# Three further expert blocks computed ahead, kept in device memory until the expert sum reaches them

## The chip, the cores and the metric

The kernel runs on one core of a Trainium2 chip. The core has a matrix engine (TensorE, PE in the profile; its weight loads are PEld), a vector engine (VectorE, DVE), an activation engine (ScalarE, ACT), GpSimd (POOL) and SyncE (SP), whose queue issues nearly all transfers between the device's memory and the on-chip memory. The metric is the device time of one execution in microseconds, as the median of several runs.

## The reference, cut to what matters

One decoder layer is computed for 1024 prompt tokens and 32 sample tokens (8 sequences of 4), 1056 columns in all, at width 1024. An RWKV-7 mixer and a pooling mixer share one input projection; their outputs go through `W_out` and are added to x, which gives h. Then comes PEER, a feed-forward part with 16384 single-neuron experts: each token has 8 heads, each head picks 16 experts by product keys, and

```
act = gelu(einsum('thkd,td->thk', u_tab[expert], xn)) * gate
out = einsum('thk,thkd->td', act, v_tab[expert])
```

with `xn = rmsnorm(h)`. A gated per-layer embedding and a final norm end the layer. All in float32.

## The kernel before, in words

Features lie on the 128 partitions, tokens along the free dimension. The column order is 32 sample tokens and then 1024 prompt tokens. The columns are worked in four groups, `GROUPS = ((0, 288), (288, 544), (544, 800), (800, 1056))`.

**Two ways to the experts.** Columns 0 to 671 (`ND = 672`) are done densely: the product of all 16384 u rows with the tokens is formed, in 128 blocks of 128 experts (`EB = 128`), multiplied by a dense gate (zero for experts not chosen) that was built in memory (`g_d`) earlier, and multiplied by the v table. Columns 672 to 1055 (384 tokens, `GT`) are done by gathers: POOL fetches the chosen u and v rows and DVE multiplies and adds them (L1229, L1237, L1246).

**A float32 product from three fast ones.** Each operand is split in a high part (ACT copy to fp32r) and a rest (a subtraction), and hi·hi, hi·lo and lo·hi are added. `esplit` (L1092 to L1099) loads 512 KB of a weight block into `eraw` (3 buffers, SP), writes `ehi` (ACT, L1096) and `elo` (2 buffers each), the latter on DVE (L1098) or, where the caller passes `PTT`, on POOL (the profile shows those at line 127). `emm` (L1120) does the matmuls: 8 pieces of the contraction, three products, two halves of 336 columns, so 48 matmuls for one block.

**One u block.** `ublock(b)` does esplit, emm into a PSUM tile `pd` (2 buffers) and a Gelu on ACT (L1126) into a 672-wide tile: `OT0` to `OT7` for the first eight (`NPRE = 8`), a rotating `wt` tile (3 buffers) for the later ones. `OT0` to `OT5` are in the pool `dr`; `OT6`, `OT7`, `wt` and the gate tile `gq` are in pools that are opened only when the pool `gp` of the dense gate is closed.

**The last group is projected.** `phase_c(gi)` adds the mixers' output projection to x, giving `h` (tile `h` of the pool `work`, 128 x 8 x 288), normalises h in place, splits it (L682 and line 127) and, for the gathered tokens, transposes it on PE (L728) into `xt_d`. After that `h` is not used. Then 16 blocks of `wq` are multiplied (`mm3`, L655 to L657), the results copied to `q` (L738, tile of `work`), multiplied with the keys (L743), and the scores go to memory (L747). It has 24 steps: 8 blocks of `w_out`, 16 of `wq`. For the last group the first 18 blocks of weights come ready split from `wc_d` by SP (L644, L645, half blocks, 3 buffers `whi` and `wlo`); from block 18 (`C3E`) on they go through `esplit` with POOL.

**What stands beside it.** At step 4 the generator of the dense gate for the last dense tile, `t_stream(2)` (top-k and selection on DVE, L765 to L860; one-hots, L905 to L907; small matmuls L913; copies L914 on ACT; 2 MB stores `g_d`, L916), is written out first; then `merge` interleaves the 24 steps of `phase_c(3)` with the 8 steps of `upre`, always taking the stream with the smaller finished share (phase_c at a tie).

**What follows.** `gtop(0)` selects experts for the first 128 gathered tokens. Then the pools of `phase_c` (`ws`, `mv`, `work`) are closed and `dw` is opened in their place, with 9 buffers each of `wh` and `wl`. `dense` walks the 128 blocks: ublock if it is not there yet, then `ugate` (multiply by the gate, L1177, DVE; high part `wh`, L1179, ACT; rest `wl`, L1181, DVE). After each eight blocks `vblock` multiplies them with eight blocks of v (L1120 again), adding into OT (L1191 for the first group, L1189 later). The first v group is written out right after block 8 of u. The gather loop and the tail (the gated embedding, for dense tokens `td`, for gathered ones `tg` with the tile `GH`) follow.

The order in each engine's queue is not the program's order: a planner lists the instructions by a simulated time, with the program's order as priority, and each engine then works its list strictly in order.

Of the kernel before, what the change touches and what calls it, by code (L numbers as in the profile page):

```python
# [10 lines left out]
F32 = mybir.dt.float32  # L11
# [4 lines left out]
AF = mybir.ActivationFunctionType  # L16
# [4 lines left out]
KB = D // 128  # L21
# [21 lines left out]
ND = GB - GA  # L43
GT = T - ND
XW = T // 3
NH = ND // 2
# [17 lines left out]
def body(ctx, tc, io):  # L64
    nc = tc.nc
    mm = nc.tensor.matmul
    TT, STT, TS, ACT = (nc.vector.tensor_tensor, nc.vector.scalar_tensor_tensor, nc.vector.tensor_scalar,
                        nc.scalar.activation)

    const = ctx.enter_context(tc.tile_pool(name="const", bufs=1))  # L70
    dram = ctx.enter_context(tc.tile_pool(name="dram", bufs=1, space=bass.MemoryType.DRAM))
# [9 lines left out]
    h2_d = dram.tile([128, KB, GT], F32, name="h2_d")  # L81
    wc_d = dram.tile([KB + 16, 128, 2, KB, 128], F32, name="wc_d")
    xt_d = dram.tile([GT, D], F32, name="xt_d")
    g_d = dram.tile([EB // GQ, 128, NTC, GQ, TC], F32, name="g_d")

    def v3(ap, n):
# [358 lines left out]
    maxn = max(b - a for a, b in GROUPS)  # L445
# [478 lines left out]
    def b_stream(ca, cb, ahead=2):  # L924
        while nxt[0] < cb or any(c < cb for c, _ in active):
            c = nxt[0]
            if (c < min(cb + ahead, NCH) and len(active) < NSLOT and (not active or since[0] >= STAG)
                    and not (held[0] and c % NSLOT == 1)):
                active.append((c, bchunk(c)))
                nxt[0], since[0] = c + 1, 0  # L930
            since[0] += 1
            for a in list(active):
                try:
                    next(a[1])
                except StopIteration:
                    active.remove(a)
                yield

    def b_len(ca, cb):
        return (cb - ca) * 19  # L940
# [6 lines left out]
    def t_stream(gi):  # L947
        for t0, m in tiles_of(gi):
            if GA <= GROUPS[gi][0] + t0 < GB:
                yield from top(tk, GROUPS[gi][0] + t0, m)  # L950

    def t_len(gi):
        n = 0
        for t0, m in tiles_of(gi):
            if GA <= GROUPS[gi][0] + t0 < GB:
                n += 24 + m // GT8
        return n

    def merge(streams):
        live = [[0, n, g] for n, g in streams]  # L960
        while live:
            s = min(live, key=lambda s: s[0] / s[1])
            try:
                next(s[2])
                s[0] += 1
            except StopIteration:
                live.remove(s)
# [101 lines left out]
    work = cstack.enter_context(tc.tile_pool(name="wc", bufs=1, reuse_waits="tile"))  # L1069
# [11 lines left out]
    def xsplit():  # L1081
        return (dr.tile([128, KB, ND], F32R, name="XH"), dr.tile([128, KB, ND], F32R, name="XL"))

    NPRE = 8
    NWT = 3
    DP = ((0, NH), (NH, NH))
    U = {}

    def PD():
        return dps.tile([128, 2, 512], F32, name="pd")  # L1090

    def esplit(src, sub=TT):  # L1092
        raw = dr.tile([128, KB, 128], F32, name="eraw", bufs=3)
        nc.sync.dma_start(raw, src)
        hi = dr.tile([128, KB, 128], F32R, name="ehi", bufs=2)
        ACT(hi, raw, AF.Copy)  # L1096
        lo = dr.tile([128, KB, 128], F32R, name="elo", bufs=2)
        sub(lo, raw, hi.bitcast(F32), op=ALU.subtract)  # L1098
        return hi, lo  # L1099
# [3 lines left out]
    def otile(db):  # L1103
        if db not in OT:
            OT[db] = (dr if db < KB - 2 else late).tile([128, ND], F32, name=f"OT{db}")
        return OT[db]

    def wt_tile():
        return late.tile([128, ND], F32, name="wt", bufs=NWT)

    def halves(t):
        return t.rearrange("p (a b) -> p a b", a=2)

    def emm(ps, w, xs, parts):
        wh_, wl_ = w
        for k in range(KB):
            xh, xl = xs[k]
            for w_, x_, first, last in ((wh_, xh, k == 0, False), (wh_, xl, False, False), (wl_, xh, False, k == KB - 1)):
                for a, (s, n) in enumerate(parts):
                    mm(ps[:, a, :n], w_[:, k, :], x_[:, s:s + n], start=first, stop=last)  # L1120

    def ublock(b, sub=TT):
        ps = PD()
        emm(ps, esplit(io["uT"][b], sub), xs, DP)
        U[b] = otile(b) if b < NPRE else wt_tile()
        ACT(halves(U[b]), ps[:, :, :NH], AF.Gelu)  # L1126

    def upre():
        for b in range(NPRE):
            ublock(b, PTT)  # L1130
            yield

    CL = [0, 24, 24, 24, 24]
    for step in range(1, NG + 1):
        streams = []
        if step < NG:
            c_ = BC[step + 2:step + 4]
            streams.append((b_len(*c_), b_stream(*c_)))
        if 0 <= step - 2 < NG:
            streams.append((t_len(step - 2), t_stream(step - 2)))  # L1140
        if 0 <= step - 1 < NG:
            streams.append((CL[step], phase_c(step - 1)))
        if step == NG:
            for _ in streams[0][1]:
                pass
            gstack.close()
            late = ctx.enter_context(tc.tile_pool(name="late", bufs=1, side="right", reuse_waits="tile"))
            gqp = ctx.enter_context(tc.tile_pool(name="gqp", bufs=2, side="right", reuse_waits="tile"))
            streams = [streams[1], (NPRE, upre())]
        merge(streams)  # L1150
        if step == NG - 1:
            nc.sync.dma_start(io["wkv_p"], S[-1])
            pbx.close()
            dr = ctx.enter_context(tc.tile_pool(name="dr", bufs=1, side="right", reuse_waits="tile"))
            dps = ctx.enter_context(tc.tile_pool(name="dps", bufs=2, side="right", space=bass.MemoryType.PSUM, reuse_waits="tile"))
            XH, XL = xsplit()
            for k in range(KB):
                nc.sync.dma_start(XH[:, k, :].bitcast(F32), xh_d[:, k, :])
                nc.sync.dma_start(XL[:, k, :].bitcast(F32), xl_d[:, k, :])
            xs = [(XH[:, k, :], XL[:, k, :]) for k in range(KB)]  # L1160
# [10 lines left out]
    def ugate(b):  # L1171
        if b % GQ == 0:
            gqs[0] = gqp.tile([128, NTC, GQ, TC], F32, name="gq")
            nc.sync.dma_start(gqs[0], g_d[b // GQ])
        wt_ = U[b]
        w3 = wt_.rearrange("p (c t) -> p c t", t=TC)
        TT(w3, w3, gqs[0][:, :, b % GQ, :], op=ALU.mult)  # L1177
        wh = dw.tile([128, ND], F32R, name="wh", bufs=VG + 1)
        ACT(wh, wt_, AF.Copy)  # L1179
        wl = dw.tile([128, ND], F32R, name="wl", bufs=VG + 1)  # L1180
        TT(wl, wt_, wh.bitcast(F32), op=ALU.subtract)  # L1181
        Ws[b] = (wh, wl)

    def vblock(g, db):
        w = esplit(io["vP"][g, db])
        ps = PD()
        emm(ps, w, [Ws[b] for b in range(g * VG, (g + 1) * VG)], DP)
        if g:
            TT(halves(OT[db]), ps[:, :, :NH], halves(OT[db]), op=ALU.add)  # L1189
        else:  # L1190
            ACT(halves(OT[db]), ps[:, :, :NH], AF.Copy)  # L1191
        if g == EB // VG // 2:
            ht = wt_tile()
            nc.sync.dma_start(ht, hT_d[:, db, GA:GB])
            TT(OT[db], OT[db], ht, op=ALU.add)

    def dense(b0, b1):
        for b in range(b0, b1):
            if b < EB:
                if b not in U:  # L1200
                    ublock(b)
                ugate(b)
            if b % VG == 0 and b:
                for db in range(KB):
                    vblock(b // VG - 1, db)

    NB0 = 2 * VG + 2
    dense(0, NB0)
    for col in range(128, GT, 128):
        gtop(col)  # L1210
# [5 lines left out]
    dpt = ctx.enter_context(tc.tile_pool(name="dpt", bufs=2, space=bass.MemoryType.PSUM, reuse_waits="tile"))  # L1216

    dense(NB0, EB + 1)

    for col in range(0, GT, 128):  # L1220
# [31 lines left out]
        for half in range(2):  # L1252
            ps = dpt.tile([128, 512], F32, name="pt")
# [3 lines left out]
            o = ht[:, half * 4:half * 4 + 4, :m]  # L1257
# [184 lines left out]
def program(arrays, extra=()):  # L1442
    nc = bacc.Bacc("TRN2", target_bir_lowering=False, num_devices=1)
    io = {k: nc.dram_tensor(k, v.shape, mybir.dt.from_np(v.dtype), kind="ExternalInput").ap()
          for k, v in arrays.items()}
    for k, s in list(OUTS.items()) + list(extra):
        io[k] = nc.dram_tensor(k, s, F32, kind="ExternalOutput").ap()
    with tile.TileContext(nc, schedule_with_timeline_sim=True) as tc, ExitStack() as ctx:
        body(ctx, tc, io)
    return nc  # L1450
# [15 lines left out]
```

## Time and profile before

| | |
|---|---|
| three runs | 3265.51, 3267.89, 3258.73 us, median 3265.51 |
| the profiled execution | 3262.93 us, span 3261.2 us |
| PE | busy 3103.6 us, 95% of the span |
| DVE | busy 2584.9 us, 79% |
| POOL, ACT | busy 1391.2 us and 1109.8 us |
| granted TensorE clock, mean | 0.973 |
| transfers | 857.86 MB, mean 263 GB/s |
| the stage that is changed | about 1110 to 1325 us |
| the dense sum | about 1325 to 3146 us, then the tail |

Busy times are shares of one engine's span and overlap between engines. The profiled execution lies 2.58 us under the median of the runs. A row of a windows table gives, for a stretch of time, its length and each engine's busy time with the number of instructions, then the granted clock, the share of the DMA engines and GB/s.

### The profile page before, as it was taken

How to read it: one execution, taken by the hardware profiler on the slowest of the kernel's cores; microseconds unless marked ns; L12 is line 12 of the kernel's file. 1: busy time of each engine (PE TensorE's matmuls, PEld its weight loads, DVE VectorE, ACT ScalarE, POOL GpSimd, SP SyncE). 2: the span in 40 equal slices, each digit the busy share in tenths (PEclk: the TensorE clock that was granted, in tenths of full speed). 3: DMA queues.
4: the chain of work that ended last, by engine and by line, in shares of the span. 5: the costliest groups of instructions: out<-in, count | busy, mean ns of one | idle time of the engine just before them, and what ended most of it. 6: DMA issues, size and time to landing. Idle time of an engine off the chain costs nothing.

```text
span 3261.2 us, 66203 instructions
## 1 busy us (share of the span) xinstructions
PE 3103.6 (95%) x26807; PEld 2983.0 (91%) x26807; DVE 2584.9 (79%) x5093; ACT 1109.8 (34%) x1708; POOL 1391.2 (43%) x1069
## 2 busy tenths in 40 slices
PE   8998899989989688999999999999999999999998
PEld 7887788878878588999999999999999999999997
DVE  7776344479998995988889888888888888888955
ACT  6442323435645554322122222222212212212343
POOL 5211410020020242156666666656666666666532
PEclk9999899999999799999999999999999999999998
DMA  3326457958877868389999999999999999999823
GB/s 119 113 95 146 129 166 220 300 164 258 252 220 231 273 214 273 126 296 337 328 346 344 317 350 343 321 339 357 324 327 346 330 331 343 337 327 342 312 97 126
DMA packets 436129, 857.86 MB, mean 263 GB/s; under 512 B 109808, under 2 KB 230896, under 8 KB 431344
## 3 DMA queue, kind: packets, MB, share of 16 engines
q1 hardware_dynamic: 324560, 447.76, 42.5%
q0 software_dynamic: 111264, 405.88, 34.4%
q8 instruction: 210, 3.44, 0.4%
q14 instruction: 95, 0.78, 0.1%
HBM read 732.92 MB, written 120.60 MB: 262 GB/s over the span
## 4 chain that ended last, share of the span: by engine, by line
PE 81%; DVE 9%; DMA 6%; ACT 2%; issue 1%; POOL 1%; SPq 0%; DVEq 0%; ACTq 0%; POOLq 0%
PE pd L1120 59%; PE ps L470 6%; PE ps L219 4%; PE ps L655 3%; PE ps L657 2%; PE ps L656 2%; DMA wlo<-wc_d 1%; PE ps L913 1%; PE ps L302 1%; DVE ab L905 1%; PE ps L1027 1%; PE ps L743 1%; DVE ab L906 1%; DVE ab L907 1%; DMA scq<-sc_d 1%
## 5 line engine op out<-in xcount | busy, mean ns | idle before, releaser
L1229 POOL DMA_INDIRECT row<-u,idx x384 | 547.9, 1427 | 310.9 <-DVE row L1237 127.5
L1096 ACT ACTIVATE ehi<-eraw 128x1024 fp32r<-128x1024 f32 x273 | 289.7, 1061 | 1127.2 <-PE pd L1120 1033.1
L1229 POOL DMA_INDIRECT row<-v,idx x384 | 534.2, 1391 | 317.3 <-DVE po L1246 143.4
L1120 PE MATMUL pd<-XH,elo 128*128 128x336 f32 x2176 | 514.9, 317 | 1.1 <-POOL elo L127 0.8
L1120 PE MATMUL pd<-XL,ehi 128*128 128x336 f32 x2176 | 515.3, 317 | 0.0
L1120 PE MATMUL pd<-XH,ehi 128*128 128x336 f32 x2176 | 512.3, 316 | 2.1 <-DVE tt L1300 2.1
L1120 PE MATMUL pd<-wh,elo 128*128 128x336 f32 (+1 forms) x2112 | 504.1, 317 | 0.4 <-DVE elo L1098 0.4
L1120 PE MATMUL pd<-wl,ehi 128*128 128x336 f32 (+1 forms) x2112 | 502.8, 317 | 1.2 <-DVE wl L1181 1.1
L1120 PE MATMUL pd<-wh,ehi 128*128 128x336 f32 (+1 forms) x2112 | 503.7, 317 | 0.0
L1246 DVE SCALAR_TENSOR_TENSOR po<-row,act,po 128x1024 f32<-128x1024 f32 x381 | 488.2, 1281 | 6.7
L1237 DVE SCALAR_TENSOR_TENSOR row<-row,xt 128x1024 f32<-128x1024 f32 x384 | 455.3, 1218 | 8.2 <-DMA xt<-xt_d 4.4
L1098 DVE TENSOR_TENSOR elo<-eraw,ehi 128x1024 fp32r<-128x1024 f32 x259 | 318.0, 1228 | 75.8 <-ACT ehi L1096 75.0
L1120 PEld LDWEIGHTS pd<-XH,elo 128*128 128x128 f32 x2176 | 373.6, 188 | 1.6 <-POOL elo L127 1.1
L1120 PEld LDWEIGHTS pd<-XH,ehi 128*128 128x128 f32 x2176 | 372.6, 189 | 2.6 <-DVE tt L1300 2.5
L1120 PEld LDWEIGHTS pd<-XL,ehi 128*128 128x128 f32 x2176 | 371.2, 188 | 0.0
L1120 PEld LDWEIGHTS pd<-wl,ehi 128*128 128x128 f32 x2112 | 362.4, 188 | 2.1 <-DVE wl L1181 2.0
L1120 PEld LDWEIGHTS pd<-wh,elo 128*128 128x128 f32 x2112 | 361.7, 188 | 0.8 <-DVE elo L1098 0.7
L1120 PEld LDWEIGHTS pd<-wh,ehi 128*128 128x128 f32 x2112 | 362.2, 188 | 0.1
L1189 DVE TENSOR_TENSOR OT<-pd,OT 128x672 f32<-128x672 f32 x120 | 102.8, 857 | 138.1 <-PE pd L1120 137.8
L655 PE MATMUL ps<-hi,whi 128*128 128x256 f32 (+1 forms) x592 | 186.3, 316 | 26.2 <-DMA whi<-wc_d 16.5
L914 ACT ACTIVATE gst<-ps 128x512 f32<-128x512 f32 x168 | 170.5, 1103 | 69.1 <-PE ps L913 67.7
L657 PE MATMUL ps<-hi,wlo 128*128 128x256 f32 (+1 forms) x592 | 182.4, 309 | 6.2 <-DMA wlo<-wc_d 5.9
(441 smaller groups left out, 5032.2 us busy)
## 6 DMA issues: line engine op xcount, KB each, us to landing
eraw<-uT SPq DMA_DIRECT2D x128, 512.0 KB, 6.3
eraw<-vP SPq DMA_DIRECT2D x128, 512.0 KB, 6.6
g_d<-gst SPq DMA_DIRECT2D x21, 2048.0 KB, 9.5
gq<-g_d SPq DMA_DIRECT2D x32, 1344.0 KB, 9.9
whi<-wc_d SPq DMA_DIRECT2D x108, 256.0 KB, 4.7
wlo<-wc_d SPq DMA_DIRECT2D x108, 256.0 KB, 4.9
fdc<-fd SPq DMA_DIRECT2D x16, 896.0 KB, 8.1
wc_d<-whi SPq DMA_DIRECT2D x40, 256.0 KB, 4.2
```

The costliest lines, as they stand in the source:

```text
L219: mm(ps[:, :XW], s[:, k, :], x[:, k, a:b], start=first, stop=last)
L470: mm(o[hs], l[hs], r[hs], start=start, stop=stop)
L655: mm(ps[:, :n], whi[:, kk, :], xhi[:, k, :n], start=k == 0, stop=False)
L657: l = mm(ps[:, :n], wlo[:, kk, :], xhi[:, k, :n], start=False, stop=k == K - 1)
L914: ACT(st[:, :, t2 + q:t2 + q + 4].rearrange("p e t -> p t e"), v3(ps, 128), AF.Copy, scale=1.0 / GS)
L1096: ACT(hi, raw, AF.Copy)
L1098: sub(lo, raw, hi.bitcast(F32), op=ALU.subtract)
L1120: mm(ps[:, a, :n], w_[:, k, :], x_[:, s:s + n], start=first, stop=last)
L1189: TT(halves(OT[db]), ps[:, :, :NH], halves(OT[db]), op=ALU.add)
L1229: nc.gpsimd.indirect_dma_start(out=r[:m], out_offset=None, in_=io[tab], in_offset=bass.IndirectOffsetOnAxis(ap=idx[:m, hh, k:k + 1], axis=0))
L1237: STT(r[:m], r[:m], 1.0, xt[:m], op0=ALU.mult, op1=ALU.mult, accum_out=pre[:m, k:k + 1])
L1246: STT(po[:m], r[:m], act[:m, k:k + 1], po[:m], op0=ALU.mult, op1=ALU.add)
```

## The change

`upre` gets three more steps between u block 5 and u block 6. Each computes one further u block (8, 9 and 10) with POOL's subtraction, applies Gelu into a third of a tile `hold`, which takes the buffer of `h` (tag `h` of the pool `work`), and stores that third (128 x 672, 344 KB) from SP into a new memory tensor `us_d`. When `dense` comes to blocks 8 to 10 it takes a `wt` tile and loads the block from `us_d` in place of computing it. The merge weight of `upre` goes from 8 to 11.

```diff
+    us_d = dram.tile([3, 128, ND], F32, name="us_d")
...
     NPRE = 8
+    NSP = 3
...
+    def uspill():
+        hold = work.tile([128, KB * maxn], F32, name="hold", tag="h")
+        for i in range(NSP):
+            ps = PD()
+            emm(ps, esplit(io["uT"][NPRE + i], PTT), xs, DP)
+            o = hold[:, i * ND:(i + 1) * ND]
+            ACT(halves(o), ps[:, :, :NH], AF.Gelu)
+            nc.sync.dma_start(us_d[i], o)
+            yield
+
     def upre():
         for b in range(NPRE):
+            if b == KB - 2:
+                yield from uspill()
             ublock(b, PTT)
             yield
...
-            streams = [streams[1], (NPRE, upre())]
+            streams = [streams[1], (NPRE + NSP, upre())]
...
     def dense(b0, b1):
         for b in range(b0, b1):
             if b < EB:
-                if b not in U:
+                if NPRE <= b < NPRE + NSP:
+                    U[b] = wt_tile()
+                    nc.sync.dma_start(U[b], us_d[b - NPRE])
+                elif b not in U:
                     ublock(b)
                 ugate(b)
```

## The prediction

> **What bounds the kernel now.** I read the page first: its span and, in part 4, the chain of work that ended last.
>
> ```profile
> span 3261.2 us, 66203 instructions
> ...
> PE 81%; DVE 9%; DMA 6%; ACT 2%; issue 1%; POOL 1%; SPq 0%; DVEq 0%; ACTq 0%; POOLq 0%
> PE pd L1120 59%; PE ps L470 6%; PE ps L219 4%; PE ps L655 3%; PE ps L657 2%; PE ps L656 2%; DMA wlo<-wc_d 1%; PE ps L913 1%; PE ps L302 1%; DVE ab L905 1%; PE ps L1027 1%; PE ps L743 1%; DVE ab L906 1%; DVE ab L907 1%; DMA scq<-sc_d 1%
> ```
>
> Four fifths of the chain is PE, and 59% of the span is the one line that multiplies with expert weights. Next the windows of 100 us from 1320 on: the first whole one, the last whole dense one, and the sum over 1320 to 3220.
>
> ```profile
> 1420.00:1520.00 100.00, 100.00 (x653) 100.00 (x652) 89.74 (x114) 21.80 (x26) 71.80 (x50) 1.00 0.94 344
> 2920.00:3020.00 100.00, 100.00 (x654) 100.00 (x653) 88.36 (x104) 24.62 (x30) 66.47 (x46) 1.00 0.94 340
> ...
> sum 1900.00, PE 1897.29 PEld 1895.79 DVE 1625.54 ACT 490.23 POOL 1135.40; mean PE 99.86 PEld 99.78 DVE 85.55 ACT 25.80 POOL 59.76
> ```
>
> PE is never idle there, at the full clock. A microsecond of PE work taken out of this stretch is a microsecond off the end, if nothing else becomes late. The stretch before it, in which the last group is projected, looks different: windows of that stage.
>
> ```profile
> 1116.00:1196.00 80.00, 70.06 (x554) 66.54 (x553) 79.56 (x270) 43.74 (x64) 38.72 (x30) 0.97 0.64 197
> 1196.00:1240.00 44.00, 38.57 (x333) 36.38 (x330) 35.69 (x126) 22.65 (x30) 4.76 (x1) 0.92 0.84 253
> 1240.00:1287.00 47.00, 38.28 (x317) 36.06 (x315) 18.94 (x50) 20.82 (x29) 10.00 (x4) 0.89 0.87 271
> 1287.00:1325.00 38.00, 35.06 (x233) 33.20 (x232) 31.45 (x111) 16.12 (x23) 6.50 (x3) 1.00 0.58 210
> ```
>
> From 1196 to 1287 PE is idle for 44.00 - 38.57 = 5.4 us and 47.00 - 38.28 = 8.7 us, and the clock granted is 0.92 and 0.89. The same two windows for line 1120 alone:
>
> ```profile
> 1196.00:1240.00 44.00, 12.73 (x63) 0.92 0.84 253
> 1240.00:1287.00 47.00, 0.67 (x5) 0.89 0.87 271
> ```
>
> Before 1240, 63 expert matmuls fill gaps; after it there are five. The code says why: with weights 24 to 8, u block 6 comes behind 19 steps of the projection and block 7 behind 22, and the split weights of wq blocks 18 to 21 hold the two `ehi` buffers ahead of block 7. With 24 to 11 the new blocks stand behind steps 14, 16 and 18, all ahead of wq block 18. They can be ready where fill is missing.
>
> **What is taken out.** The price of a block comes from one piece of the chain:
>
> ```profile
> 1321.75 128.31 PE pd L1120 x831
> ```
>
> 128.31 / 831 = 0.1544 us for a matmul, so 48 x 0.1544 = 7.41 us for a block and 22.2 us for three. The dense sum loses that, and three subtractions on DVE. Nothing is saved by it as such: the same 144 matmuls now stand earlier in the same queue. The gain is the PE idle time and slow clock that they use up, less new idle time.
>
> **What they can use up.** The idle time is 5.4 + 8.7 = 14.1 us. The missing clock is 8% of 44 us with PE busy 88% of it, 3.1 us, and 11% of 47 us with PE busy 81%, 4.2 us. Together 21.4 us: the upper bound, nearly the size of the three blocks. The lower bound is 0, since a queue worked in order keeps its waits when work is added in the wrong places. Such waits, in order of time on PE:
>
> ```profile
> 1231.38 0.39 PE L655 MATMUL ps<-hi,whi 128*128 128x256 f32 x1 [1.55 <-DMA whi<-wc_d]
> ...
> 1250.74 1.67 PE L913 MATMUL ps<-ab 128*128 128x128 f16 x14 [2.48 <-DVE ab L907]
> ...
> 1254.67 0.58 PE L657 MATMUL ps<-hi,wlo 128*128 128x256 f32 x1 [1.59 <-DMA wlo<-wc_d]
> ```
>
> The first lies in the window that had fill. So fill does not remove all: 5.4 us in 44 stayed, which is 5.8 us in 47. If the second window comes to look like the first, it gives 8.7 - 5.8 + 4.2 = 7.1 us; if it is filled whole, 8.7 + 4.2 = 12.9 us. I take 10.0 us, between the two, and keep 0 and 21.4.
>
> The clock row bears on this.
>
> ```profile
> 1250.00:1260.00 10.00, 7.27 (x46) 6.66 (x47) 5.65 (x16) 4.06 (x4) 0.13 (x1) 0.50 0.88 258
> ```
>
> [...]
>
> **What loses its cover.** Block 8 stands before the first v group now, and its second half runs where PE would otherwise wait:
>
> ```profile
> 1306.39 1.28 PE L743 MATMUL ps<-keys,q 128*128 128x128 f32 x10
> ...
> 1320.49 0.57 PE L1120 MATMUL pd<-wl,ehi 128*128 128x336 f32 x2 [0.28 <-DVE wl L1181]
> ```
>
> ```profile
> L1120 PE MATMUL pd<-wh,ehi x36: 309/317/322, 1311.2 to 1329.8; 128*128 128x336 f32 x36
> ...
> L1179 ACT ACTIVATE wh<-OT x8: 752/754/757, 1308.2 to 1312.8; 128x672 fp32r<-128x672 f32 x8
> L1181 DVE TENSOR_TENSOR wl<-OT,wh x8: 834/850/859, 1309.0 to 1319.6; 128x672 fp32r<-128x672 f32 x8
> ```
>
> The last score matmul ends at 1307.67. Only then may `wh` use the projection's memory, and the eighth `wl` is done at 1320.45; the first v block waits for it. Between the score and the first v matmul at 1311.2 PE does the last 24 matmuls of block 8, 24 x 0.1544 = 3.7 us. They are gone, and the v block still ends with the eighth `wl`. So 3.7 us of new idle time; 0 if DVE orders these subtractions closer. I take 3.7. Blocks 9 and 10 leave from between the first and second v group, where DVE keeps up: its mean share is 85.55%, and it has three subtractions less.
>
> **The rest of the new work.** Where the new blocks wait for `h`, its last readers are long done (the transposes, to 1191.8). POOL's subtraction is slow but POOL has time (4.76 of 44, 10.00 of 47).
>
> ```profile
> L728 PE MATMUL ps<-ident,h x16: 270/273/329, 1177.8 to 1191.8; 128*128 128x128 f32 x16
> ```
>
> ```profile
> L127 POOL TENSOR_TENSOR elo<-eraw,ehi x14: 2373/2862/4759, 1114.9 to 1296.4; 128x1024 fp32r<-128x1024 f32 x14
> L1126 ACT ACTIVATE OT<-pd x8: 711/730/732, 1132.1 to 1296.2; 128x672 f32<-128x672 f32 x8
> L1126 ACT ACTIVATE wt<-pd x8: 709/714/737, 1314.4 to 1425.7; 128x672 f32<-128x672 f32 x8
> ...
> hT_d<-h SPq DMA_DIRECT2D x8, 128.0 KB, 4.5
> ...
> gq<-g_d SPq DMA_DIRECT2D x4, 1344.0 KB, 8.8
> ```
>
> Per block: 2.9 us on POOL in place of 1.2 on DVE, the same 0.73 us of ACT, the same 512 KB load, only earlier. New are a store and a load of 344 KB, each between 4.5 and 8.8 us by its neighbours, say 5.5. The loads of blocks 8 to 10 need their `wt` tiles by the second v group, some 59 us (eight v blocks) after the first begins: hidden, 0. Without that cover they would cost 5.5 us once, being issued together. The three `wt` buffers go round as before.
>
> The stores are the dangerous part. SP waits until the Gelu is done, and the weight halves for the projection are queued behind it. The waits of SP in that stage:
>
> ```profile
> SPq L731 <- ACT xt L730: 18.2, 4, 10.7
> ...
> SPq L916 <- ACT gst L914: 9.9, 5, 3.6
> ```
>
> A store that waits for ACT has held SP for 9.9 / 5 = 2.0 us on the mean, or 18.2 / 4 = 4.6. Three stores: 5.9 to 13.7 us of SP, which counts only where a weight half is due. The planner places a store by the time at which it expects the Gelu; I take 0 beyond the waits that the 10 us leave in, and keep 13.7 for a rival.
>
> [...]
>
> **The end.** The gathers start from the scores of the projection. Half of block 8 already stands ahead of the last score matmul, so 22.2 - 3.7 = 18.5 us of work come in before it, and it ends 18.5 - 10.0 = 8.5 us later; the dense sum then ends 14.8 us (blocks 9 and 10) less that 8.5 earlier. The two come 14.8 us closer together.
>
> ```profile
> L1281 ACT ACTIVATE wh<-GH,vecs x8: 599/610/617, 3132.1 to 3139.3; 128x384 fp32r<-128x384 f32 x8
> ...
> L1266 ACT ACTIVATE rg<-GH x1: 527/527/527, 3115.9 to 3115.9; 128x384 f32<-128x384 f32 x1
> ```
>
> The gathered result is there at 3115.9; the first use that must follow the dense sum is at 3132.1. That is 16.2 us of room, so 1.4 is left and the price is 0; with DVE's idle 14% the gathers may catch up besides. Without that room it would be the part of 14.8 that is over.
>
> **The sum.** -10.0 + 3.7 = -6.3 us. On the profiled execution, 3262.93, that is 3256.6; on the median, 2.58 us higher at 3265.51, it is 3259.2. The likeliest case's own range is 3252 to 3266 (12.9 saved without new idle time, or 7.1 saved with 3.7 lost and a few us of run to run spread). This kernel's runs lie 9.2 us apart, so I count changes of up to 0.3%, 9.8 us, as none.
>
> **The rivals.** *The stage swallows the blocks whole*: all 21.4 us used, 3.7 lost, -17.7 us, 3247.8. For it: in the second window ACT, POOL and DVE are busy less than half the time, so a block finds its split weights ready. Against: the waits in the window that had fill.
>
> *The blocks only push the projection back*: 0 used, 3.7 lost, 3269.2. For it: the new blocks stand ahead of later wq blocks in program order, so the planner prefers them to the projection rather than using them as fill, and the projection is what ends the stage. Against: the half clock from 1250 to 1260, where nothing is ready.
>
> *The stores hold the weights*: SP stands at a store before its Gelu, the halves behind it are late, and PE, in order, waits with them. Nothing used, 3.7 lost, 13.7 us of SP stalls handed on: +17.4 us, 3282.9, slower. It decides from the point where the stalls handed on exceed the 6.3 us of gain, 2.1 us a store; to be seen as slower they need 16.1, or 6.1 with nothing used. For it: the 18.2 us of waits at L731. Against: those waits were at tiles with one buffer in turn, and `hold` has three thirds.
>
> **How the numbers follow.** Forecast 0.45, swallowed 0.22, pushed back 0.18, stores 0.15. Faster by over 0.3% is all of the second (0.22) and the upper part of the forecast's range, some 0.13: 0.35. Slower by over 0.3% is the stores (0.15) and a little of the pushed-back case: 0.17. The rest is 0.48. The range takes in the first three cases with the spread of the runs, 3245 to 3276, and leaves most of the stores' case out.
>
> **What would show it.** Right: after 1240 dozens of expert matmuls among the projection's, in place of five; the last score matmul some 8.5 us later; the first `wh` right behind it, and PE idle some 4 us more around the first v block; two u blocks fewer between the first and second v group; no wait of the second v group on `wt`; the full clock through the stage. Wrong: SP rows of the new stores (from `hold`) with waits over 2 us followed by PE waits on `whi` or `wlo`; the last score matmul 18 us later with the idle time unchanged; PE waiting for the gathered result near 3130.

## The result, and the profile after

Seven runs of the changed kernel have a median of 3278.79 us (3274.63 to 3284.63), beside 3263.95 us for the kernel before on the same chip. It is 14.8 us slower by these medians and some 18 us by the ratio of the runs, 1.0056, whose 95% interval is 1.0043 to 1.0068. The forecast was 3259.2 us, 6.3 us less than before, with a range of 3245 to 3276.

First the page of the changed kernel, its span and chain of work:

```profile
span 3276.4 us, 66203 instructions
...
PE 56%; DVE 2%; DMA 1%; issue 1%; ACT 0%; POOL 0%; DVEq 0%; SPq 0%; ACTq 0%; POOLq 0%
```

The span grew by 15.2 us. The shares fell because the chain of after could be followed back only about as far as the changed stage; they are not to be set beside those of before. A first whole window of the dense sum looks as it did, PE never idle at the full clock:

```profile
1420.00:1520.00 100.00, 100.00 (x653) 100.00 (x652) 90.58 (x117) 23.25 (x28) 61.77 (x45) 1.00 0.87 316
```

So the time is lost ahead of the dense sum or behind it. Two windows of the stage, after (columns as in the prediction):

```profile
1196.00:1240.00 44.00, 35.86 (x323) 34.19 (x322) 35.58 (x102) 24.20 (x32) 2.72 (x2) 0.96 0.81 241
1240.00:1287.00 47.00, 34.18 (x268) 32.24 (x266) 17.94 (x47) 17.16 (x23) 4.75 (x2) 0.85 0.88 286
```

The same two for line 1122, which was line 1120:

```profile
1196.00:1240.00 44.00, 14.91 (x79) 12.47 (x78) 0.96 0.81 241
1240.00:1287.00 47.00, 9.41 (x52) 8.42 (x50) 0.85 0.88 286
```

The new matmuls are where they were expected: 52 after 1240 in place of five. But PE is idle for 47.00 - 34.18 = 12.8 us in the second window, where it was 8.7, and the clock is 0.85, where it was 0.89. The fill went in and the gaps grew.

To compare two executions the clock times must be aligned, since executions of the same queues differ by some microseconds before the stage begins: the mark used here stands at 1045.3 to 1065.0 us in the profiled executions. It is the issue of the store `wkv_p`, the last one ahead of the stage; everything before it is the same in both kernels. The groups of instructions of that tile and of the score matmuls, after:

```profile
L1166 SPq DMA_DIRECT2D wkv_p<-S x1: 382/382/382, 1051.3 to 1051.3; - x1
...
L744 PE MATMUL ps<-keys,q x64: 270/275/581, 1228.3 to 1333.2; 128*128 128x128 f32 x64
```

and before:

```profile
L1152 SPq DMA_DIRECT2D wkv_p<-S x1: 382/382/382, 1051.8 to 1051.8; - x1
...
L743 PE MATMUL ps<-keys,q x64: 271/275/377, 1222.3 to 1307.4; 128*128 128x128 f32 x64
```

The last score matmul starts 281.9 us after the mark instead of 255.6: 26.3 us later. 18.5 of it are the 120 matmuls that now stand ahead of it (144 less the 24 of block 8 that stood there already); the rest, 7.8 us, is new. The whole stretch from the mark to the end of the last score, before and then after:

```profile
1051.80:1307.70 255.90, 206.86 (x1650) 192.02 (x1649) 205.16 (x725) 122.35 (x171) 68.38 (x49) 0.87 0.80 256
1051.30:1333.50 282.20, 222.46 (x1767) 208.43 (x1766) 208.03 (x728) 127.60 (x178) 70.05 (x52) 0.89 0.75 241
```

PE is idle for 59.7 us in place of 49.0, 10.7 us longer. It is busy for 15.6 us longer, 2.9 us less than the 18.5 us of added work, at a mean clock of 0.89 instead of 0.87. So 10.7 - 2.9 = 7.8 us. The waits of PE from 1110 on (waiting line, releaser, us in total, times, longest), after:

```profile
PE ps L656 <- DMA whi<-wc_d: 20.3, 5, 6.7
PE pd L1122 <- DVE tt L1317: 6.6, 1, 6.6
PE pd L1122 <- DVE XL L1299: 2.6, 1, 2.6
PE ps L658 <- DMA wlo<-wc_d: 1.5, 2, 1.1
```

and before, the same window and then 3100 to 3200:

```profile
PE ps L655 <- DMA whi<-wc_d: 4.8, 4, 1.6
PE ps L657 <- DMA wlo<-wc_d: 3.1, 3, 1.6
...
PE pd L1120 <- DVE tt L1300: 2.1, 1, 2.1
```

Two items grew: waits for the projection's weight halves, 7.9 to 21.8 us, and waits in the tail, here 2.1 to 6.6 + 2.6 = 9.2 (9.9 with a third wait of 0.7). PE's timeline shows the three long waits for halves (start, length, instruction; in brackets the idle time before it and its releaser):

```profile
1215.67 0.39 PE L656 MATMUL ps<-hi,whi 128*128 128x256 f32 x1 [4.63 <-DMA whi<-wc_d]
...
1274.39 0.58 PE L656 MATMUL ps<-hi,whi 128*128 128x256 f32 x1 [6.71 <-DMA whi<-wc_d]
...
1290.06 0.55 PE L656 MATMUL ps<-hi,whi 128*128 128x256 f32 x1 [6.20 <-DMA whi<-wc_d]
```

Together 17.5 us. The first stands before the first store to `us_d` is issued (1220.42). The other two hang together, as the timeline of SP's queue shows:

```profile
1263.72 0.37 SPq L917 DMA_DIRECT2D g_d<-gst  x1
1264.20 5.24 SPq L645 DMA_DIRECT2D whi<-wc_d  x1
...
1273.39 0.73 SPq L1188 DMA_DIRECT2D gq<-g_d  x1
...
1277.00 1.00 SPq L1216 DMA_DIRECT2D wt<-us_d  x2
1278.37 0.32 SPq L645 DMA_DIRECT2D whi<-wc_d  x1
```

and PE's timeline beside it:

```profile
1277.67 0.41 PE L658 MATMUL ps<-hi,wlo 128*128 128x256 f32 x1
```

By their order, the half that PE gets at 1274.39 is the one issued at 1264.20. It arrives late, 10.2 us after its issue, so the matmuls on it end late, at 1278.08; only then is its buffer free, and the next half is asked for at 1278.37. By then the gate's loads (`gq`, 1344 KB) and the new `wt` loads are on their way, and that half is used from 1290.06 on, 11.7 us after its issue. Before, the last pair of halves was issued ahead of such loads:

```profile
1271.48 0.73 SPq L644 DMA_DIRECT2D whi<-wc_d  x1
...
1274.55 0.79 SPq L1174 DMA_DIRECT2D gq<-g_d  x2
```

One window inside the stage of after adds the clock:

```profile
1270.00:1280.00 10.00, 4.74 (x19) 4.15 (x19) 0.00 (x0) 0.98 (x2) 0.27 (x1) 0.53 1.00 307
```

PE is idle for 5.26 of these 10 us, the DMA engines are never free (1.00), and the granted clock is 0.53.

The tail. The first matmul of the gated embedding follows the last one of the dense sum. Line 1122 from 3100 to 3200, after and then before:

```profile
L1122 PE MATMUL pd<-XH,ehi x59: 311/316/648, 3145.7 to 3200.0; 128*128 128x336 f32 x59
```

```profile
L1120 PE MATMUL pd<-XH,ehi x80: 311/315/482, 3138.4 to 3197.0; 128*128 128x336 f32 x80
```

The dense sum ends 7.3 us later (7.8 aligned), and the span 15.2: half the loss is in the last 130 us. The chain of work over that part, after and then before:

```profile
3101.45 1.04 DVE po L1263
...
3133.93 6.71 DMA GH<-h_d
...
3169.56 74.72 PE pd L1122 x452
```

```profile
3104.95 41.50 PE pd L1120 x269
```

Before, the chain runs through PE. After, from 3101 to 3170 it leaves PE for the gathers (`po`), their last transfers and the vector work on `GH`. The groups of that tile, after:

```profile
L1298 ACT ACTIVATE wh<-GH,vecs x8: 600/603/605, 3144.6 to 3150.9; 128x384 fp32r<-128x384 f32 x8
...
L1283 ACT ACTIVATE rg<-GH x1: 527/527/527, 3140.7 to 3140.7; 128x384 f32<-128x384 f32 x1
```

The gathered result is there at 3140.7 instead of 3115.9, 24.8 later, and the first `wh` from it comes 3.9 us after that; before it had 16.2.

### The profile page after: what moved, and what is told of

Its sections match the earlier page's. It is cut to its first block, busy times and chain, and to the rows that moved or that the text cites. A ratio compares the mean times of both kernels' runs of the same rounds, so it can differ in the third digit from the quotient of the medians.

```text
span 3276.4 us, 66203 instructions
## 1 busy us (share of the span) xinstructions
PE 3101.4 (95%) x26807; PEld 2981.7 (91%) x26807; DVE 2585.9 (79%) x5090; ACT 1109.8 (34%) x1708; POOL 1399.3 (43%) x1072
## 4 chain that ended last, share of the span: by engine, by line
PE 56%; DVE 2%; DMA 1%; issue 1%; ACT 0%; POOL 0%; DVEq 0%; SPq 0%; ACTq 0%; POOLq 0%
PE pd L1122 56%; DVE po L1263 0%; DVE XL L1299 0%; DVE wl L1299 0%; DVE OT L1354 0%; DMA sc_d<-scs 0%; DMA GH<-h_d 0%; DVE elo L1100 0%; DMA h_d<-row 0%; DVE GH L1354 0%; DMA scq<-sc_d 0%; ACT ehi L1098 0%; POOL elo L128 0%; ACT tg L1285 0%; PE pt L1335 0%
## 5 line engine op out<-in xcount | busy, mean ns | idle before, releaser
L1246 POOL DMA_INDIRECT row<-v,idx x384 | 541.3, 1410 | 321.3 <-DVE po L1263 135.0
L656 PE MATMUL ps<-hi,whi 128*128 128x256 f32 (+1 forms) x592 | 185.2, 314 | 39.9 <-DMA whi<-wc_d 33.3
```

Source lines behind the costliest of these rows:

```text
L656: mm(ps[:, :n], whi[:, kk, :], xhi[:, k, :n], start=k == 0, stop=False)
L1246: nc.gpsimd.indirect_dma_start(out=r[:m], out_offset=None, in_=io[tab], in_offset=bass.IndirectOffsetOnAxis(ap=idx[:m, hh, k:k + 1], axis=0))
```

## The experiments

Twelve kernels. One profiled execution each is read from the mark `wkv_p`: the start of the last score matmul and its length, and the end of the span. Beside it stand the median, and the ratio to the kernel before on the same chip. That kernel's median was 3259.65 us beside the rows from "stores out" to "before, weight 11", 3261.56 beside the four with short gathers or resident halves, and 3258.14 beside the last four. Waits for halves are counted from 1110 us on. Aligned numbers come from single executions and differ from what the medians say by up to 9.7 us (late loads: 7.3 and 17.0); where the two disagree the text names both.

| kernel | median us | ratio, interval | end of last score | end of span | PE waits for halves | PE waits in the tail |
|---|---|---|---|---|---|---|
| before | 3263.95 | | 255.9 | 2209.4 | 7.9 | 2.1 |
| after | 3278.79 | 1.0056, 1.0043 to 1.0068 | 282.2 | 2225.1 | 21.8 | 9.9 |
| stores out | 3282.34 | 1.0067, 1.0046 to 1.0088 | 280.9 | 2224.5 | 22.0 | 9.5 |
| stores and loads out | 3274.34 | 1.0047, 1.0032 to 1.0062 | 275.9 | 2219.2 | 17.2 | 9.2 |
| loads after the last half | 3276.61 | 1.0035, 1.0017 to 1.0052 | 273.2 | 2216.7 | 15.1 | 8.1 |
| before, weight 11 | 3273.32 | 1.0034, 1.0019 to 1.0049 | 263.5 | 2216.6 | 15.0 | 2.1 |
| before, short gathers | 3259.49 | 0.9989, 0.9972 to 1.0005 | 254.5 | 2208.2 | 7.9 | 2.1 |
| after, short gathers | 3270.76 | 1.0028, 1.0014 to 1.0042 | 281.9 | 2217.1 | 20.4 | 2.1 |
| before, halves resident | 3244.39 | 0.9952, 0.9933 to 0.9971 | 238.9 | 2188.2 | 0.4 | 2.1 |
| after, halves resident | 3251.88 | 0.9973, 0.9960 to 0.9987 | 256.9 | 2202.7 | 0 | 9.4 |
| after, weight 8 | 3255.75 | 1.0008, 0.9994 to 1.0022 | 253.5 | 2207.1 | 10.1 | 2.1 |
| after, one block | 3262.10 | 1.0009, 0.9999 to 1.0019 | 260.0 | 2208.3 | 16.8 | 2.1 |
| three whole weight blocks | 3248.66 | 0.9970, 0.9957 to 0.9982 | 243.3 | 2195.7 | 5.5 | 2.1 |
| five whole weight blocks | 3243.24 | 0.9953, 0.9936 to 0.9969 | 239.3 | 2189.8 | 4.1 | 2.1 |

### The stores taken out

The new blocks are computed as in after, but not stored; blocks 8 to 10 are loaded from other data of the same size.

```diff
-            nc.sync.dma_start(us_d[i], o)
...
-                    nc.sync.dma_start(U[b], us_d[b - NPRE])
+                    nc.sync.dma_start(U[b], hT_d[:, b - NPRE, GA:GB])
```

> The changed kernel without the three stores of the new blocks; blocks 8 to 10 are loaded from a slice of the same size of another tensor, so their values are left out. Theory 'stores hold the weights' (my third rival): the 20 us of PE waits on whi fall under 8 us and the time falls by 10 to 15 us, to 3264 to 3269. Theory 'new blocks stand ahead of the projection': the stores never waited (0.4 to 0.7 us each in the queue), so the time stays within 4 us of 3278.8 and the last score matmul stays near 1333.

Nothing came back: 1.0067 beside 1.0056, the last score 1.3 us sooner, the waits for halves 22.0. The stores of after say why, as groups of instructions (ns shortest/median/longest, then first and last start):

```profile
L1136 ACT ACTIVATE hold<-pd x3: 712/732/732, 1219.0 to 1267.8; 128x672 f32<-128x672 f32 x3
L1137 SPq DMA_DIRECT2D us_d<-hold x3: 422/465/720, 1220.4 to 1272.9; - x3
```

These stores held SP for 0.4 to 0.7 us. The planner put each behind its Gelu; the last comes 4 us after it. The third rival, stores that hold the weights, falls.

### Stores and loads taken out

As above, and blocks 8 to 10 filled with a constant in place of the load, so that no transfer is new.

```diff
-            nc.sync.dma_start(us_d[i], o)
...
-                    nc.sync.dma_start(U[b], us_d[b - NPRE])
+                    nc.gpsimd.memset(U[b], 0.01)
```

> The changed kernel with neither the three stores nor the three loads; blocks 8 to 10 are filled with a constant by POOL in place of the load, so their values are left out. Theory 'transfers collide' (the 2 MB that the change adds make the last weight halves late): the two PE waits of 6.7 and 6.2 us on whi near 1274 and 1290 shrink by half or more and the time falls by 8 to 15 us. Theory 'new blocks stand ahead of the projection': at most 4 us fall away, and the last score matmul stays later than 1326, 18.5 us of work after the 1307.7 of the kernel before.

The last score comes 6.3 us sooner than in after and the waits for halves fall from 21.8 to 17.2, but by the ratios (1.0047, 1.0056) only some 3 us of the loss of 14.8 go, and the intervals overlap. With no new transfer at all the kernel is still slower by 0.47%, and PE still waits once for 7.3 us for a half.

### The late loads kept behind the last half

The loads of the gate and of the three blocks may be issued only after the last half of the projection's weights.

```diff
-    wraws = {}
+    wraws, lastw = {}, {}
...
-                nc.sync.dma_start(lo.bitcast(F32), wc_d[b, :, 1, ks, :])
+                lastw[0] = nc.sync.dma_start(lo.bitcast(F32), wc_d[b, :, 1, ks, :]).ins
...
-            nc.sync.dma_start(gqs[0], g_d[b // GQ])
+            with tc.issue_after(lastw[0]):
+                nc.sync.dma_start(gqs[0], g_d[b // GQ])
...
-                    nc.sync.dma_start(U[b], us_d[b - NPRE])
+                    with tc.issue_after(lastw[0]):
+                        nc.sync.dma_start(U[b], us_d[b - NPRE])
```

> The changed kernel with the loads of the gate tiles and of the new blocks put behind the last weight load of the projection in SP's queue. Theory 'transfers collide': the wait of 6.2 us near 1290 goes, the projection ends 5 to 10 us sooner, near 1325, the time falls to 3266 to 3273. Theory 'new blocks stand ahead': the time is within 4 us of 3278.8, or up to 10 us longer because the gate tiles come late and the first v group waits for them.

In the profiled execution the waits for halves are 15.1 us instead of 21.8 and the last score comes 9.0 us sooner. The runs do not bear this out clearly: the ratio is 1.0035 instead of 1.0056, about 7 us, but the intervals overlap, and by the medians the kernel is still 17.0 us slower than before. So the trace suggests that the collision of late halves with those loads is one part of the loss; the times do not show it. The larger rest stands, with one wait of 6.8 us among it.

### The merge weight alone

The kernel before, with no new block and no new transfer, only with the weight of `upre` at 11.

```diff
-            streams = [streams[1], (NPRE, upre())]
+            streams = [streams[1], (NPRE + 3, upre())]
```

> The kernel before with only the merge weight of the u blocks ahead changed from 8 to 11: no new blocks, no new transfers. Theory 'the new order, not the new work, costs the time': the last score matmul moves from 1307.7 to 1315 or later and the time rises by 5 to 12 us over the kernel before. Theory 'the new work costs it': within 4 us of the kernel before, or faster, since the blocks 6 and 7 get ahead of the wq blocks that held their buffers.

PE's waits in this kernel, from 1110 on:

```profile
PE ps L655 <- DMA whi<-wc_d: 12.9, 4, 5.1
PE ps L657 <- DMA wlo<-wc_d: 2.1, 2, 1.4
```

This one number makes the kernel slower by 0.34% (0.19 to 0.49), 11 us by the ratio, 13.7 by the medians and 7.2 aligned. The waits for halves double, 7.9 to 15.0, the last score comes 7.6 us later, and neither amount of work nor transfer has changed. Only the order has: the eight u blocks are asked for earlier among the projection's steps, block 5 behind 11 of them instead of 16. In the changed kernel blocks 0 to 5 stand just as early, since its weight is 11 too. Line 1120 (1122 in after) from the mark to the last transposition, before, weight 11 and after:

```profile
1051.80:1192.10 140.30, 46.14 (x267) 41.79 (x268) 0.84 0.79 249
1065.00:1214.00 149.00, 53.81 (x307) 48.63 (x307) 0.87 0.75 239
1051.30:1197.70 146.40, 54.22 (x307) 48.96 (x308) 0.87 0.76 241
```

Forty more expert matmuls stand ahead of the transpositions in both, 40 x 0.1544 = 6.2 us of work, and the transpositions end 8.7 and 6.1 us later. What follows is that matmuls written ahead of the projection's are preferred to them rather than used as fill. That the halves then come later because their three buffers are freed later by the delayed matmuls is what the rows of after at 1274 to 1290 show once; for the sum of the waits it was not tested by itself.

### Shorter gathers, before and after

The gather of the last 128 tokens leaves out one head of eight, so that the gathered result is there sooner; done to both kernels.

```diff
-        for hh in range(HEADS):
+        for hh in range(HEADS - 1 if col == 256 else HEADS):
```

> The kernel before without the gathers and sums of the last head of the last 128 gathered tokens (32 of 768 gathers left out), so that the gathered result is there some 70 us earlier. It is the base for the next run. Both theories: the end was not set by the gathers, so within 4 us of the kernel before.

> The changed kernel with the same 32 gathers left out. Theory 'the gathered result is late at the end': the PE waits between the dense sum and the first gate (9.9 us in the changed kernel, 2.1 in the kernel before) fall to about 2 and the time falls by 7 to 8 us; against the run with the same gathers left out of the kernel before, 7 to 9 us remain, all from the projection's stage. Rival 'the planner's order of the tail is worse by itself': the 9.9 us stay and so does the whole difference of 15 us.

Before, it changes nothing that can be told (0.9989, 0.9972 to 1.0005): the gathers had room. After, the tail's waits fall from 9.9 to 2.1 us and the span from 2225.1 to 2217.1, while the last score stays (281.9, 282.2). So 8.0 us aligned of the loss are the gathers at the end. With both shortened the difference is 2217.1 - 2208.2 = 8.9 us instead of 15.7; by the medians 3270.76 - 3259.49 = 11.3 instead of 14.8.

### The halves resident, before and after

After the first wq block of the last group, the blocks that come ready split all reuse that one block's weights, so that their halves are not loaded at all; done to both kernels.

```diff
+        if gi == NG - 1 and b > KB:
+            return wraws["one"]
-        out = []
+        out = wraws["one"] = []
```

> The kernel before with the weights of the first wq block used for the next nine blocks of the last group as well, so that their 18 half loads fall away (their values are left out). Base for the next run. PE waited 7.9 us for weight halves in this stage: the projection ends 8 to 15 us sooner and the time falls by as much.

> The changed kernel with the same loads left out. Theory 'the new blocks make the projection's weight halves late' (PE waited 21.8 us for them, against 7.9): the time falls by 20 to 28 us, and against the run before it is within 6 us, the tail's loss being left. Rival 'the new blocks push the projection whether its weights come or not': the difference to the run before stays at 14 us or more.

Both gain, after the more: by the ratios 0.48% before and 1.0056 to 0.9973 after, some 16 and 27 us; the last score 17.0 and 25.3 us sooner. So the halves cost after 8.3 us more (11 by the ratios), which agrees with the 7.8 us that are new in the stage. What remains is the price of the blocks where hardly any half is late: the last score 256.9 - 238.9 = 18.0 us later, for 18.5 us of work. From the mark to the end of that score, before and then after:

```profile
1046.80:1285.70 238.90, 198.96 (x1648) 187.26 (x1648) 202.12 (x726) 122.27 (x171) 65.37 (x49) 0.89 0.73 236
1055.10:1312.00 256.90, 216.72 (x1767) 203.45 (x1766) 210.53 (x727) 126.99 (x178) 70.85 (x52) 0.91 0.71 227
```

PE is idle for 39.9 and 40.2 us. The blocks added no idle time there, and they used none. Aligned, the span keeps 14.5 us of difference, by the medians 7.5; the profiled executions are the fastest and the slowest of their ten runs, so the 7.5 counts. It lies between what the theory (within 6) and the rival (14 or more) had expected. The tail's waits are 9.4 us, among them

```profile
PE pd L1124 <- DVE tt L1319: 5.9, 1, 5.9
```

so the loss at the end does not need late halves: here it came with a last score that was 18.0 us later and a dense sum that had two blocks less to do.

### The three blocks at the old weight, and one block alone

After with the merge weight of before, and after with only block 8 spilled (weight 9):

```diff
-            streams = [streams[1], (NPRE + NSP, upre())]
+            streams = [streams[1], (NPRE, upre())]
```

> The changed kernel with the merge weight back at 8 for its 11 steps: u blocks 0 to 5 stand where they stood in the kernel before, the new blocks behind steps 19 and 22 of the projection and after its end. Theory 'blocks that stand ahead of the projection's wq blocks make its weight halves late': the PE waits for halves fall from 21.8 us to 8 to 12, the last score matmul comes 8 us or more sooner than in the changed kernel, and the time falls by 8 to 15 us, to 3264 to 3271. Rival 'any new block in this stage costs its full length': within 4 us of 3278.8.

```diff
-    NSP = 3
+    NSP = 1
```

> The changed kernel with one new block in place of three (merge weight 9). If the loss is one of order and lateness, a step and not a slope, it keeps more than half of its 15 us: 3271 to 3276. If each block costs alike, a third: 3266 to 3270. If the first block fits into idle time and only the later ones do not: at or under the kernel before, 3255 to 3264.

With weight 8 the loss is gone, below what even the theory expected, and there is no gain: 1.0008 (0.9994 to 1.0022). PE's waits for halves are nearly those of before, 10.1 us. The last score comes at 253.5 (255.9 before), the first v matmul at 271.1 (259.4). Nearly all the new work stands behind the projection now: 115 expert matmuls, 17.6 us, lie between the last score and the first v matmul, where 24, 3.5 us, lay before, and the dense sum has two blocks less to do. The tail's room is kept. So the same three blocks with the same transfers cost nothing when they do not stand ahead of the projection and blocks 1 to 5 are not drawn forward. The two went together here; new blocks ahead with the old ones left in place were not run.

With one block at weight 9 the ratio is 1.0009 (0.9999 to 1.0019). The time, 3262.10 us, lies where the third expectation put it, but the block did not fit into idle time: the last score is 4.1 us later, for the 24 matmuls (3.7 us) that moved ahead of it. The waits for halves are 16.8 us, more than double, and the time hardly shows it. So the sum of these waits is not by itself the price. The tail loses nothing.

### The idle tile as a weight buffer

If halves that come late are what costs, the idle tile `h` may be better used for them. In the kernel before, with no expert block added, some of the split wq blocks are loaded whole (1 MB, both parts in one transfer) into that tile: three of them (blocks 10, 13, 16), or five as shown.

```diff
+        if gi == NG - 1 and b in (9, 11, 13, 15, 17):
+            big = work.tile([128, 2, KB, 128], F32R, name="wbig", tag="h")
+            nc.sync.dma_start(big.bitcast(F32), wc_d[b])
+            return [(big[:, 0, s], big[:, 1, s]) for s in (slice(0, HK), slice(HK, KB))]
```

> The kernel before, without new blocks; the idle tile of h takes whole weight blocks instead: wq blocks 10, 13 and 16 of the last group are loaded into it in one 1 MB transfer each, and the three half buffers serve the other blocks. Theory 'the projection is held by its weight halves' (without 18 of the 20 loads the kernel before was 17 us faster): three blocks of ten stop waiting for a half buffer, the last score matmul comes 4 to 10 us sooner, the time falls to 3251 to 3260. Rival 'the transfers themselves are the limit, not the buffers': within 4 us of the kernel before.

> The same with five blocks through the idle tile of h: 9, 11, 13, 15 and 17, every other one. Theory 'the buffers hold the projection': 6 to 14 us sooner than the kernel before, 3248 to 3258, better than with three. Rival 'the transfers themselves are the limit': within 4 us of the kernel before, or slower, since each 1 MB block must land whole before its first matmul and the tile is free only once the block before it is multiplied.

The first is faster by 0.30% (0.18 to 0.43), the second by 0.47% (0.31 to 0.64), 3243.24 us (four runs) beside 3258.14 on the same chip. Both lie below what was expected, and the rival, transfers as the limit, falls. With five the last score comes 16.6 us sooner than before, nearly all of the 17.0 that resident weights gave, and the tail's waits are 2.1 us as before. This kernel is faster than both before and after.

## Why the prediction was wrong

In its own terms the prediction was -10.0 (idle time used) + 3.7 (lost cover) + 0 (tail) = -6.3 us. Measured on the same terms, aligned: +7.8 + 0 + 7.9 = +15.7.

**What bounds the kernel: right.** The dense sum is PE at the full clock, before and after. The first v matmul, after:

```profile
L1122 PE MATMUL pd<-wh,ehi x22: 310/316/422, 1334.8 to 1344.5; 128*128 128x336 f32 x22
```

From it to the first of the tail, 1311.2 to 3138.4 became 1334.8 to 3145.7: 16.3 us less, of which 14.8 are blocks 9 and 10, as priced.

**What they can use up: the step that failed first.** The bounds were 0 and 21.4 us, and 10.0 was taken; the value is -7.8, below the lower bound. Of the 14.1 us of idle time none was used, and 10.7 us came on top; of the missing clock, put at 7.3 us, 2.9 us came back. The prediction read idle time of PE as room. It is room only for work that comes when nothing of the projection is ready. These blocks stood ahead of the projection's last steps in program order, and in a queue worked in order that is before them, not in their gaps. The trace of after shows PE keep its order: it stood 6.20 us at the half of 1290.06, while the split weights of the matmuls that it took next, from 1290.62 on (`ps<-hi,ehi`), were written by 1270.27. Nor did the prediction follow its "24 to 11" to the end: it placed the three new blocks by it and left out that blocks 1 to 5 move forward as well. The lower bound was argued as "a queue worked in order keeps its waits when work is added in the wrong places"; the waits were not kept, they grew, from 7.9 to 21.8 us for halves. That the order alone makes the last score late by about as much (7.6 us), the weight 11 kernel shows; that new loads beside late halves add to it is only suggested by the trace with the late loads. Even with the halves resident 18.0 of the 18.5 us stayed, and with the blocks behind the projection PE is idle for 24.6 us from 64.0 us after the mark to the end of the last score, beside 25.4 us before. So no run shows idle time that was used. The second rival had this mechanism in its "for it" and put the price at 0 used. What the prediction itself said of the program order spoke for it, and it was given 0.18. The clock row was read too readily: it shows 0.50 beside waits of 2.48 and 1.59 us, and the one of after 0.53 beside a wait of 6.71 us, but not which wait lowers the clock. That filled gaps bring it back was the author's estimate, and no run shows a gap that was filled: over the stage the mean rose from 0.87 to 0.89, but from 1240 to 1287 it fell from 0.89 to 0.85 with 52 expert matmuls in place of five.

**What loses its cover: mis-sized, 3.7 taken, 0 measured.** The bounds were right and the lower one came true, for the reason given there: DVE ordered the subtractions closer. DVE's timeline, after:

```profile
1334.76 5.47 DVE L1195 TENSOR_TENSOR wl<-OT,wh 128x672 fp32r<-128x672 f32 x7 [1.77 <-ACT wh L1193]
1343.64 0.49 DVE L766 MAX8 V<-scq 128x8 f32<-128x128 f32 x2 [3.41 <-DMA scq<-sc_d]
```

Seven subtractions follow each other directly; before, the top-k of the last scores stood between them up to 1320.45. After, that top-k has to wait for its scores until 1343.6. The first v matmul starts 1.3 us behind the last score instead of 3.5, and the first v blocks wait 1.5 us less.

**The rest of the new work: right, with one size off.** POOL, ACT and the loads of the three blocks delay nothing of the dense sum; PE never waits for `wt`. The median landing, issues from 1260 to 1300 of after:

```profile
wt<-us_d SPq DMA_DIRECT2D x3, 336.0 KB, 11.6
gq<-g_d SPq DMA_DIRECT2D x3, 1344.0 KB, 9.6
whi<-wc_d SPq DMA_DIRECT2D x5, 256.0 KB, 6.4
```

A load of 344 KB (336 as the profile counts) took 11.6 us where 5.5 was taken: loads of 1344 KB were on their way at the same time. It was hidden behind its 59 us of cover all the same. What the prediction left out is the other side of it: the halves that were still to come took 6.4 us to land, beside 4.3 us for the two in the same stretch of before.

**The stores: right that they cost nothing, wrong as a rival.** They held SP for at most 0.72 us each, not 2.0 to 4.6, and without them the time is the same (1.0067 beside 1.0056). The sign this rival gave was right, its mechanism was not: what the halves met were not these stores but their own late order and, by the trace, the loads.

**The end: the second step that failed.** The two ends were to come 14.8 us closer, with 16.2 us of room. That was drawn from a projection 8.5 us later. It came 26.3 us later, and the gathered result 25.3 us (aligned), while the dense sum ended only 7.8 us later. So the result came 17.5 us closer to the end of the dense sum, and the hope that the gathers "may catch up" in DVE's idle 14% was not borne out. The waits of 9.9 us instead of 2.1 follow from this: the short gathers take them away. The room was mis-sized too. It was measured to the first use of the result, but in after, in both kernels without stores and in the one with late loads, each with waits of 8.1 us or more in the tail, that use comes 3.8 to 3.9 us after the result, beside 16.0 us with weight 11. Of the 16.2 us only about 12.3 were room, and the planned 14.8 was already more. By this 17.5 - 12.3 = 5.2 of the 7.8 us of new waiting are accounted for; the other 2.6 us are open.

**The signs.** Of those named as right, the dozens of matmuls after 1240 came, the first `wh` right behind the last score, two u blocks fewer between the first and second v group, and no wait on `wt`; the time of the last score, the idle time at the first v block and the full clock did not. Of those named as wrong, two came: the last score later by more than 18 us with the idle time not reduced, and PE waiting for the gathered result.

## What to carry to other kernels

Idle time of an engine is not room for other work until it is known what it waits for and which work the order prefers: here the filler was placed ahead of the work that waited, and its waits grew from 7.9 to 21.8 us, while the same blocks behind it cost nothing and gained nothing. A merge weight that is changed to place new work moves the old work too; alone it cost 0.34%. Look at what a stage's late end sets going (here gathers that had about 12 us of room at the other end of the kernel) and subtract the whole delay, not the planned one. Before giving a free buffer to more work, ask whether the wait that makes the gap would go away with that buffer: as a place for weights the same tile was worth 0.47%.

## What was not expected of the hardware

From 1190 on the issue that follows a 2 MB store of the dense gate (`g_d`) on SP took 5.2 to 6.8 us instead of some 0.4. In SP's timeline of after, above, the half issued behind the store of 1263.72 took 5.24 us; a pair of before:

```profile
1243.15 0.67 SPq L916 DMA_DIRECT2D g_d<-gst  x1
1243.91 5.80 SPq L645 DMA_DIRECT2D wlo<-wc_d  x1
```

The four such stores were followed by issues of 6.81, 5.38, 5.80 and 5.75 us before, and of 5.34, 5.71, 5.96 and 5.24 us after. The half issued at 1264.20 in after landed after 10.2 us, the next two after 6.2 and 6.3. No run took these stores away, so what they cost the projection is open; the half that PE gets at 1274.39 in after was issued behind one, and the half that it gets at 1215.67 behind a store of `xt_d` that was held 5.34 us behind another.

Profiled executions reached the mark `wkv_p` between 1045.3 and 1065.0 us with the same queues ahead of it. So a difference of a few microseconds between two spans says nothing until the executions are aligned, and the verdicts rest on the times of all runs. Left open as well: the idle time that is left in the stage with resident halves, which no run could fill, and how the 7.8 us divide between the order and the collision of transfers. The order alone gave 7.6 and keeping the loads back gave 9.0 at the last score, which together is more than there was.
